# Output projection of a hybrid attention/SSD layer: four token blocks interleaved over each weight block, two at the start of the second half of the columns

## The chip, the cores and the metric

The kernel runs on one core of a Trainium2 chip. A core has five engines with an instruction stream each: TensorE (PE, with its weight loads PEld), VectorE (DVE), ScalarE (ACT), GpSimd (POOL) and SyncE (SP), whose queue issues the DMA transfers here. Matmuls write their sums into PSUM, which has eight banks of 128 x 512 values of 32 bits; other data lies in SBUF. The metric is the device time of one execution in microseconds, as the median of several runs.

## The reference

One layer over 1024 tokens of width 1024: a combined input projection, differential attention, a Mamba-2 SSD branch, and at the end the two branches are merged by gates and projected back.

```python
merged = jax.nn.sigmoid(g_a) * (y_a @ w_proj_attn) + jax.nn.sigmoid(g_s) * (y_s @ w_proj_ssd)
return x + (merged @ w_out).astype(x.dtype)
```

All of it is float32. The change concerns only the last product, `merged @ w_out`, of 1024 x 1024 by 1024 x 1024, and the addition of x.

## The kernel before, in words

A float32 operand is split into a high and a low part of a faster format (F32R): ScalarE writes the high part, VectorE or GpSimd subtracts it for the low part (`act` at L224, `tt` at L232). A product is then three matmuls, high x high, high x low, low x high (`steps3`), all recorded by `mm` at L198.

The program records its instructions through a planner (`Plan`): tasks are Python generators that run in an order set by modelled costs and due times, and each engine executes what was recorded for it in that order. Waits between engines are semaphores set by the framework from the real uses of the buffers. The planner decides the order, the chip decides the times.

The stages before the projection are the three products that give `merged` (`products`, tiles pX, pY, pZ, with the gates gl and the partial results ac). `merged` stands transposed, in blocks of 128 channels by 512 tokens: `mgs[kb, half]`, kb from 0 to 7, each with high and low part. They lie in whatever buffers were free, so in the rows they are called mg, hH or hL; for a part of them an `acc_d` block is read back and split in place.

The projection is `final`. Its loop is over two halves n of the 512 output columns; in each, over eight token blocks t of 128; in each, over the eight weight blocks kb of 128 rows by 512 columns. One weight block is one tile `w` with a high and a low part; w136 to w143 are those of the first half, w144 to w151 those of the second. There are nine buffers for them and four for the raw weights as loaded (`raw`). A token block sums 8 x 3 = 24 matmuls in one PSUM bank (`po` + n + t + part), and `out_evac` then has VectorE multiply by 0.5 and add the block of x (`xr`, L240), which is stored from there (`out`). The last block of all is done in two parts of 256 columns. The weight buffers of a half come free (`w_done`) while its last token block, t = 7, passes. `XAHEAD` = 3 blocks of x are loaded ahead. PSUM banks are handed out from one ring of eight (`trs`).

Of the kernel before, what the change touches and what calls it, by code (L numbers as in the profile page):

```python
# [15 lines left out]
P = 128  # L16
S = 1024
D = 1024
KB = D // P
NT = S // P  # L20
# [15 lines left out]
ZF, ZH = {5: 2, 9: 3}, {}  # L36
WPOOL = 3
XAHEAD = 3
HOP = 0.12
INF = float("inf")  # L40

# [36 lines left out]
class Plan:  # L78
# [8 lines left out]
    def op(self, eng, cost, after, shared=False):  # L87
# [3 lines left out]
        if shared:  # L91
            self.e["L"] = s + cost
        return s + cost + HOP

# [44 lines left out]
def tile_hybrid_layer(ctx: ExitStack, tc: tile.TileContext, x, norm_w, w_in, q_norm_w, k_norm_w,  # L139
# [26 lines left out]
    pl = Plan()  # L166
    bigs, mids, sms = Slots(NBIG), Slots(NMID), Slots(NSM)
    trs, qlos = Slots(8), Slots(2)
# [8 lines left out]
    def midt(shape=(P, 512), dt=F32, name="m"):  # L177
        return mid.tile(list(shape), dt, tag="b2", name=name)
# [7 lines left out]
    def trt(name):  # L186
        return ps_tr.tile([P, 512], F32, tag="tr", name=name)

    mmt = trt
# [7 lines left out]
    def mm(o, lhsT, rhs, start, stop, after=0.0, **kw):  # L197
        nc.tensor.matmul(o, lhsT=lhsT, rhs=rhs, start=start, stop=stop, **kw)  # L198
        n, m = rhs.free_size(), lhsT.free_size()
        if rhs.dtype == F32:  # L200
            c = max(4 * n / 2400, 0.215)
        else:
            c = max(n / 2400 + lag[0], 0.057 if m <= 64 else 0.107)
        pl.t = max(pl.t, after) + c
# [5 lines left out]
    def pe_done():  # L210
        return pl.t + 0.2
# [11 lines left out]
    def act(o, i, f, after, **kw):  # L223
        nc.scalar.activation(o, i, f, **kw)  # L224
        if f in (AF.Silu, AF.Exp) and f != table[0]:
            table[0] = f
            pl.op("A", 1.3, after)
        c = 0.83e-3 * i.free_size() + (0.052 if in_ps(i) else 0.093) + 0.093 * (("accum_out" in kw) + any(not isinstance(kw.get(i, 0.0), float) for i in ("scale", "bias")))
        return pl.op("A", c, after)

    def tt(o, a, b, op, after, eng="V"):
        (nc.vector if eng == "V" else nc.gpsimd).tensor_tensor(out=o, in0=a, in1=b, op=op)  # L232
        n = o.free_size()
        if eng == "G":
            return pl.op("G", 0.095 + (1.85e-3 if op == ALU.mult else 2.3e-3) * n, after, True)
        sb = not in_ps(a, b)
        return pl.op("V", 0.07 + 0.07 * sb + 1.042e-3 * n, after, sb)

    def stt(o, a, s, b, op0, op1, after):
        nc.vector.scalar_tensor_tensor(out=o, in0=a, scalar=s, in1=b, op0=op0, op1=op1)  # L240
        sb = not in_ps(a, b)
        return pl.op("V", 0.07 + 0.07 * sb + 1.042e-3 * o.free_size() + (0.0 if isinstance(s, float) else 0.06), after, sb)
# [9 lines left out]
    def load(o, i, after=0.0):  # L252
        nc.sync.dma_start(out=o, in_=i)  # L253
        q = pl.op("Q", 0.48, max(after, pl.t))
        n = o.free_size() * 512 / 360e3 if o.space != bass.MemoryType.DRAM else i.free_size() * 512 / 360e3
        return pl.op("D", n, q + 0.6) + lag[1]
# [218 lines left out]
    def w_next(n):  # L475
        i = used[0]
        used[0] += n
        return list(range(i, i + n))

    def w_need(i):  # L480
        while i not in w_at:
            yield pl.t + 0.1
        while w_at[i] > pl.t:
            yield w_at[i]

    def w_done(i):
        ws.give(w_slot[i], pl.t + 0.1)
        wts.pop(i)

    def wide(i):  # L490
        return wts[i][:, 0].rearrange("p f c -> p (f c)"), wts[i][:, 1].rearrange("p f c -> p (f c)")
# [5 lines left out]
    def steps3(o, a, b, first, last, **kw):  # L497
        mm(o, a[0], b[0], first, False, **kw)
        yield
        mm(o, a[0], b[1], False, False, **kw)  # L500
        yield
        mm(o, a[1], b[0], False, last, **kw)
        yield
# [22 lines left out]
    def form_evac(t):  # L526
# [16 lines left out]
        def split(f, src, at):  # L543
# [4 lines left out]
            for kp in range(2):  # L548
                at = tt(forms_t[f, 1, kp][0][:, :, cs], src[:, 2 * kp:2 * kp + 2], forms_t[f, 0, kp][0][:, :, cs],
                        ALU.subtract, at - HOP if kp else at)  # L550
            forms_at[f] = at
# [20 lines left out]
    def prep_h(t):  # L572
# [24 lines left out]
        for i in range(2):  # L597
            hs = slice(i * 512, i * 512 + 512)
            at = stt(xt[:, hs], xt[:, hs], rs, nwb[i], ALU.mult, ALU.mult, at - HOP if i else at)
            nt.append(at)  # L600
# [10 lines left out]
    def h_evac(t, half, pt, kt, at):  # L611
# [5 lines left out]
        if t >= 4:  # L617
            km = yield from pl.get(mids)
            b = midt([P, 4, P], name=f"b{half + 1}2{t}")
            t1 = act(b, src, AF.Copy, at - HOP)  # L620
            sums12[t, half] = (b, km, t1)
# [86 lines left out]
    def qk_stack(h, half, qk):  # L708
# [10 lines left out]
        for isk in range(2):  # L719
# [17 lines left out]
            for m, (own, other) in enumerate(((lo, hi), (hi, lo))):  # L737
                if isk:
                    t1 = tt(kk[m][other, cs], pt[own], kk[m][own, cs], ALU.subtract, t1 - HOP)
                else:  # L740
                    t1 = stt(ql[own, m], pt[own], wqk_c[own], qh[own, m], ALU.mult, ALU.subtract, t1 - HOP)
            done.append(t1)
# [651 lines left out]
    forms, mgs = {}, {}  # L1394
# [233 lines left out]
    def final():  # L1628
        outs = [(n, t) for n in range(2) for t in range(NT)]
        for i in range(XAHEAD):  # L1630
            pl.spawn(load_xr(*outs[i]))
        for n in range(2):
            ids = w_next(KB)
            for t in range(NT):
                if n * NT + t + XAHEAD < len(outs):
                    pl.spawn(load_xr(*outs[n * NT + t + XAHEAD]))
                tsl = slice(t % 4 * P, (t % 4 + 1) * P)
                parts = 2 if (n, t) == (1, NT - 1) else 1
                for i in range(parts):
                    wsl = slice(i * 512 // parts, (i + 1) * 512 // parts)  # L1640
                    k = yield from pl.get(trs, first=True)
                    pm = mmt(f"po{n}{t}{i}")
                    for kb in range(KB):
                        yield from w_need(ids[kb])
                        while (kb, t // 4) not in mgs:
                            yield pl.t + 0.1
                        mg, at = mgs[kb, t // 4]
                        if at > pl.t:
                            yield at
                        wh, wl = wide(ids[kb])  # L1650
                        yield from steps3(pm[:, wsl], (mg[:, 0, tsl], mg[:, 1, tsl]), (wh[:, wsl], wl[:, wsl]),
                                          kb == 0, kb == KB - 1)
                        if t == NT - 1 and i == parts - 1:
                            w_done(ids[kb])
                    pl.spawn(out_evac(pm, k, xrs[n, t], slice(t * P, (t + 1) * P), n * 512, wsl, i == parts - 1), pe_done())

    xrs = {}

    def load_xr(n, t):
        xrs[n, t] = cell = []  # L1660
        km = yield from pl.get(mids)
        xt = midt(name=f"xr{n}{t}")
        cell += [xt, km, load(xt, xv[t * P:(t + 1) * P, n * 512:n * 512 + 512])]

    def out_evac(pm, k, cell, rows, c0, wsl, last):
        at = pe_done()
        while len(cell) < 3:
            yield pl.t + 0.1
        xt, km, tx = cell
        at = max(at, tx)  # L1670
        yield at
        at = stt(xt[:, wsl], pm[:, wsl], 0.5, xt[:, wsl], ALU.mult, ALU.add, at)
        trs.give(k, at)
        yield at
        at = load(ov[rows, c0 + wsl.start:c0 + wsl.stop], xt[:, wsl], at)
        if last:
            mids.give(km, at)
# [7 lines left out]
    def bulk():  # L1685
        pl.spawn(ssd_all())
        pl.spawn(prepare())
        step = {"z": ssd_proj_z, "h": att_proj}
        for kind, i in ORDER1:
            if kind in "cg":  # L1690
                yield from front_pair(kind, i, (kind, i) == FPAIRS[-1])
            elif kind in step:
                yield from step[kind](i)
            else:
                yield from dt_proj() if kind == "dt" else att_setup()
        pl.spawn(fill())
        yield from gates()
        lag[:] = [0.0135, 2.5]
        for c in range(3):
            yield from products(c)  # L1700
        yield from final()
# [58 lines left out]
```

## Time and profile before

| | us |
|---|---|
| median of 3 runs (1653.99 to 1654.98) | 1654.75 |
| the profiled execution, its own time | 1649.99 |
| its span, from the first to the last instruction | 1648.3 |
| TensorE busy in that span | 1598.3 |
| mean granted clock of TensorE, as a share of full | 0.992 |

The profile is of one further execution; its span is 1.69 us shorter than its own time, and its time is 4.76 us below the median of the runs. Matmuls are pipelined: a row's duration is longer than the distance to the next one's start, so the pace is read from starts. TensorE's granted clock has two levels, 1.2 and 2.4 GHz; 1.00 in a row of the windows is the upper one, 0.50 the lower.

### The profile page before, as it was taken

Reading aid. Unit: us, or ns where it says so; the run is one execution under the profiler, and the core shown is the slowest. Engines: PE = TensorE matmul, PEld = TensorE weight load, DVE = VectorE, ACT = ScalarE, POOL = GpSimd, SP = SyncE. Lnnn points to the kernel's source line nnn. Section 1 sums busy time; section 2 is a strip of 40 time slices with the busy share of each in tenths; the row PEclk is TensorE's granted clock in tenths of the full one; section 3 lists DMA queues with packets and bytes.
Section 4 is the critical chain, followed back from the end, with each engine's and each line's share of the span. In section 5 each row is a group of like instructions: output and inputs, shape, how many; then the busy total and the mean of one; then the engine's idle time right before and its main releaser. Section 6 shows DMA issues by size and latency. Waiting matters only on the chain. (4 is left out here: it accounts for less than half of the span.)

```text
span 1648.3 us, 24347 instructions
## 1 busy us (share of the span) xinstructions
PE 1598.3 (97%) x8010; PEld 1332.0 (81%) x8010; DVE 1082.8 (66%) x2011; ACT 911.5 (55%) x2215; POOL 701.8 (43%) x847
## 2 busy tenths in 40 slices
PE   7999999999999999999999999999999999989899
PEld 5788888888788888887878888888787887777687
DVE  7836568447782676876777877776656657796821
ACT  7534457455663557786666877676665625252410
POOL 4315455235541545456475555464665233313100
PEclk9999999999999999999999999999999999999999
DMA  6213343524452361426253514242425649596832
GB/s 207 91 57 107 108 150 107 168 87 118 132 187 82 107 203 56 129 70 180 83 192 122 152 50 133 71 156 88 145 86 190 225 132 373 184 332 205 273 128 71
DMA packets 223804, 236.47 MB, mean 143 GB/s; under 512 B 15285, under 2 KB 155326, under 8 KB 223678
## 3 DMA queue, kind: packets, MB, share of 16 engines
q1 hardware_dynamic: 223678, 234.93, 44.8%
q8 instruction: 63, 1.03, 0.3%
q14 instruction: 63, 0.52, 0.1%
HBM read 164.48 MB, written 70.39 MB: 142 GB/s over the span
## 5 line engine op out<-in xcount | busy, mean ns | idle before, releaser
L198 PE MATMUL pma<-w,hH 128*128 128x512 f32 x1024 | 346.1, 406 | 5.6 <-POOL w L232 5.4
L232 POOL TENSOR_TENSOR rawf<-rawf,rawf 128x512 f32<-128x512 f32 x90 | 121.4, 1349 | 257.6 <-DVE wp L232 110.3
L198 PEld LDWEIGHTS pma<-w,hH 128*128 128x128 f32 x1024 | 189.2, 190 | 40.4 <-POOL w L232 6.6
L198 PE MATMUL pma<-w,hL 128*128 128x512 f32 x512 | 207.5, 405 | 0.0
L224 ACT ACTIVATE wp<-rawf 128x512 fp32r<-128x512 f32 x180 | 109.4, 625 | 103.3 <-POOL rawf L232 70.3
L198 PE MATMUL pmz<-w,hH 128*128 128x512 f32 x512 | 164.3, 398 | 0.7 <-ACT hH L224 0.6
L232 DVE TENSOR_TENSOR wp<-rawf,wp 128x512 fp32r<-128x512 f32 x144 | 110.5, 787 | 55.9 <-ACT wp L224 55.7
L224 ACT ACTIVATE w<-raw 128x512 fp32r<-128x512 f32 (+1 forms) x122 | 74.8, 626 | 80.1 <-PE po L198 35.9
L224 ACT ACTIVATE p<-p,nm 128x256 f32<-128x256 f32 (+7 forms) x128 | 98.6, 773 | 32.5 <-DVE nm L771 31.7
L198 PEld LDWEIGHTS pmz<-w,hH 128*128 128x128 f32 x512 | 96.5, 190 | 20.7 <-ACT hH L224 1.0
L198 PEld LDWEIGHTS pma<-w,hL 128*128 128x128 f32 x512 | 97.3, 190 | 16.3 <-issue 0.2
L198 PE MATMUL fYc<-ft,wp 128*128 128x512 f32 x432 | 106.5, 392 | 0.7 <-DVE fu L232 0.7
L232 POOL TENSOR_TENSOR w<-raw,w 128x512 fp32r<-128x512 f32 (+1 forms) x38 | 51.5, 1355 | 124.7 <-ACT w L224 124.6
L198 PE MATMUL pmz<-w,hL 128*128 128x512 f32 x256 | 101.3, 396 | 0.0
L198 PEld LDWEIGHTS fYc<-ft,wp 128*128 128x128 f32 x432 | 81.1, 189 | 18.0 <-DVE fu L232 1.1
L232 POOL TENSOR_TENSOR s<-rawf,rawf 128x512 f32<-128x512 f32 x30 | 40.5, 1351 | 118.8 <-DMA rawf<-in_w_proj_ssd_dram 56.1
L232 DVE TENSOR_TENSOR w<-raw,w 128x512 fp32r<-128x512 f32 (+1 forms) x84 | 67.1, 810 | 23.0 <-ACT w L224 22.6
L224 ACT ACTIVATE ab<-ab,nac 128x128 f32<-128x128 f32 x256 | 78.4, 393 | 1.7 <-POOL ab L1174 1.5
L198 PEld LDWEIGHTS av<-v,at 128*128 128x128 f32 x576 | 72.8, 191 | 6.5 <-ACT at L224 2.6
L264 POOL TENSOR_TENSOR rs<-rs,mhalf 128x4 f32<-128x4 f32 (+1 forms) x71 | 75.3, 1061 | 5.9
L771 DVE CUSTOM_DVE_ANT_0 p<-sc,maskb 128x512 f32<-128x512 f32 (+3 forms) x128 | 72.1, 585 | 8.4 <-issue 4.0
L198 PE MATMUL av<-v,at 128*128 128x128 f32 x576 | 75.1, 275 | 1.5 <-ACT at L224 1.5
(301 smaller groups left out, 4074.7 us busy)
## 6 DMA issues: line engine op xcount, KB each, us to landing
raw<-in_w_in_dram SPq DMA_DIRECT2D x104, 256.0 KB, 3.5
rawf<-in_w_in_dram SPq DMA_DIRECT2D x72, 256.0 KB, 3.9
ab<-act_d SPq DMA_DIRECT2D x32, 512.0 KB, 4.7
cv_d<-cv SPq DMA_DIRECT2D x48, 256.0 KB, 2.2
t_d<-ts SPq DMA_DIRECT2D x24, 512.0 KB, 3.2
z_d<-zs SPq DMA_DIRECT2D x32, 256.0 KB, 2.0
xr<-cv_d SPq DMA_DIRECT2D x32, 256.0 KB, 3.1
zc<-z_d SPq DMA_DIRECT2D x32, 256.0 KB, 3.1
```

The costliest lines, as they stand in the source:

```text
L198: nc.tensor.matmul(o, lhsT=lhsT, rhs=rhs, start=start, stop=stop, **kw)
L224: nc.scalar.activation(o, i, f, **kw)
L232: (nc.vector if eng == "V" else nc.gpsimd).tensor_tensor(out=o, in0=a, in1=b, op=op)
L264: nc.gpsimd.tensor_tensor(out=dst, in0=dst, in1=mhalf[:, 0:cols], op=ALU.pow)
L771: nc.vector.tensor_tensor_reduce(out=p[:, j:e], in0=sc[i][:, 0:e - j], in1=maskb[:, S - n + j:S - n + e], scale=-1.0, scalar=nms[i - 1] if ...
```

## The change

In each half of the columns the token blocks are now taken in groups (`FINAL_T`): in the first half blocks 0 to 3 as one group and then 4 to 7 singly, in the second half blocks 0 and 1 as one group and then 2 to 7 singly. In a group each block has a PSUM bank of its own, and the loop over weight blocks is outside that over the group's token blocks: a weight block is used by all of them before the next is needed. The blocks of x for a whole group are asked for at the group's start. Each block is evicted after its own last matmul. The number of matmuls, loads, splits and stores stays the same.

```diff
+FINAL_T = (((0, 1, 2, 3), (4,), (5,), (6,), (7,)), ((0, 1), (2,), (3,), (4,), (5,), (6,), (7,)))
...
-            for t in range(NT):
-                if n * NT + t + XAHEAD < len(outs):
-                    pl.spawn(load_xr(*outs[n * NT + t + XAHEAD]))
-                tsl = slice(t % 4 * P, (t % 4 + 1) * P)
-                parts = 2 if (n, t) == (1, NT - 1) else 1
+            for ts in FINAL_T[n]:
+                for t in ts:
+                    if n * NT + t + XAHEAD < len(outs):
+                        pl.spawn(load_xr(*outs[n * NT + t + XAHEAD]))
+                parts = 2 if (n, ts[-1]) == (1, NT - 1) else 1
                 for i in range(parts):
                     wsl = slice(i * 512 // parts, (i + 1) * 512 // parts)
-                    k = yield from pl.get(trs, first=True)
-                    pm = mmt(f"po{n}{t}{i}")
+                    pms = []
+                    for t in ts:
+                        k = yield from pl.get(trs, first=True)
+                        pms.append((trt(f"po{n}{t}{i}"), k))
                     for kb in range(KB):
                         yield from w_need(ids[kb])
...
+                        for t, (pm, k) in zip(ts, pms):
...
+                            yield from steps3(pm[:, wsl], (mg[:, 0, tsl], mg[:, 1, tsl]), (wh[:, wsl], wl[:, wsl]),
+                                              kb == 0, kb == KB - 1)
+                            if kb == KB - 1:
+                                pl.spawn(out_evac(pm, k, xrs[n, t], slice(t * P, (t + 1) * P), n * 512, wsl, i == parts - 1),
+                                         pe_done())
+                        if ts[-1] == NT - 1 and i == parts - 1:
                             w_done(ids[kb])
-                    pl.spawn(out_evac(pm, k, xrs[n, t], slice(t * P, (t + 1) * P), n * 512, wsl, i == parts - 1), pe_done())
```

TensorE, at the start of the projection, before: one bank (po000, token block 0) takes all eight weight blocks in turn, then the next bank begins.

```order
L198 MATMUL po000_16120<-w136_16040,hH_111 128x512 x3
L198 MATMUL po000_16120<-w137_16051,hL_112 128x512 x3
L198 MATMUL po000_16120<-w138_16067,hH_111 128x512 x3
L198 MATMUL po000_16120<-w139_16079,hL_112 128x512 x3
L198 MATMUL po000_16120<-w140_16156,hH_111 128x512 x3
L198 MATMUL po000_16120<-w141_16159,hL_112 128x512 x3
L198 MATMUL po000_16120<-w142_16162,mg60_16056 128x512 x3
L198 MATMUL po000_16120<-w143_16165,hL_112 128x512 x3
L198 MATMUL po010_16190<-w136_16040,hH_111 128x512 x3
```

The same place of the change: a weight block goes through four banks, po000 to po030, before the next one.

```order
L199 MATMUL po000_16120<-w136_16040,hH_111 128x512 x3
L199 MATMUL po010_16121<-w136_16040,hH_111 128x512 x3
L199 MATMUL po020_16122<-w136_16040,hH_111 128x512 x3
L199 MATMUL po030_16123<-w136_16040,hH_111 128x512 x3
L199 MATMUL po000_16120<-w137_16051,hL_112 128x512 x3
L199 MATMUL po010_16121<-w137_16051,hL_112 128x512 x3
L199 MATMUL po020_16122<-w137_16051,hL_112 128x512 x3
L199 MATMUL po030_16123<-w137_16051,hL_112 128x512 x3
L199 MATMUL po000_16120<-w138_16067,hH_111 128x512 x3
```

So the first use of w140 moves from the 13th matmul of the stage to the 49th, and that of w143 from the 22nd to the 85th.

SP's queue behind the loads of w140 to w143's raw weights, before (raw144 to raw147 are the first four weight blocks of the second half, xr the blocks of x, out_0_dram the stores):

```order
L253 DMA raw143_16102<-in_w_out_dram 128x512
L253 DMA xr00_16123<-in_x_dram 128x512
L253 DMA xr01_16125<-in_x_dram 128x512
L253 DMA xr02_16127<-in_x_dram 128x512
L253 DMA xr03_16129<-in_x_dram 128x512
L253 DMA raw144_16170<-in_w_out_dram 128x512
L253 DMA raw145_16175<-in_w_out_dram 128x512
L253 DMA raw146_16180<-in_w_out_dram 128x512
L253 DMA raw147_16185<-in_w_out_dram 128x512
L253 DMA xr04_16192<-in_x_dram 128x512
L253 DMA out_0_dram<-xr00_16123 128x512
```

The same place of the change:

```order
L254 DMA xr03_16132<-in_x_dram 128x512
L254 DMA xr04_16134<-in_x_dram 128x512
L254 DMA xr05_16136<-in_x_dram 128x512
L254 DMA xr06_16138<-in_x_dram 128x512
L254 DMA raw144_16210<-in_w_out_dram 128x512
L254 DMA raw145_16218<-in_w_out_dram 128x512
L254 DMA raw146_16223<-in_w_out_dram 128x512
L254 DMA raw147_16228<-in_w_out_dram 128x512
L254 DMA raw148_16252<-in_w_out_dram 128x512
L254 DMA out_0_dram<-xr00_16126 128x512
L254 DMA out_0_dram<-xr01_16128 128x512
```

Three loads of x stand ahead of raw144 that stood behind raw147 before. On TensorE everything ahead of the projection stands as it stood; on ScalarE, VectorE and GpSimd the whole order is the same (each weight split, merged split and eviction at its old place).

## Rows read from the trace of the kernel before

**Rows 1.** The page: the span, and TensorE's busy time, share and instructions.

```profile
span 1648.3 us, 24347 instructions
PE 1598.3 (97%) x8010; PEld 1332.0 (81%) x8010; DVE 1082.8 (66%) x2011; ACT 911.5 (55%) x2215; POOL 701.8 (43%) x847
```

**Rows 2.** TensorE's waits from 1405 us on: releaser, total, times, longest.

```profile
PE po L198 <- DVE w L232: 3.1, 1, 3.1
PE po L198 <- ACT w L224: 2.4, 1, 2.4
```

**Rows 3.** The chain that ended last, its end: start, us, what.

```profile
1557.55 0.61 DVE w L232
...
1558.20 86.61 PE po L198 x395
...
1644.84 0.42 DVE xr L240
```

**Rows 4.** Timeline of TensorE in the projection: start, us, operation, count, idle before.

```profile
1549.31 0.84 PE L198 MATMUL po<-w,hH 128*128 128x512 f32 x3
...
1554.56 0.50 PE L198 MATMUL po<-w,hH 128*128 128x512 f32 x1 [2.36 <-ACT w L224]
1558.20 1.22 PE L198 MATMUL po<-w,hH 128*128 128x512 f32 x2 [3.14 <-DVE w L232]
1559.22 1.48 PE L198 MATMUL po<-w,hL 128*128 128x512 f32 x3
1560.50 1.48 PE L198 MATMUL po<-w,mg 128*128 128x512 f32 x3
...
1562.69 0.85 PE L198 MATMUL po<-w,hH 128*128 128x512 f32 x3
...
1595.34 4.24 PE L198 MATMUL po<-w,mg 128*128 128x512 f32 x18
...
1606.24 0.84 PE L198 MATMUL po<-w,hH 128*128 128x512 f32 x3
```

**Rows 5.** Windows: busy time and count of each engine, TensorE's clock, DMA share, GB/s.

```profile
1050.43:1052.51 2.08, 2.08 (x10) 1.69 (x9) 1.64 (x6) 1.47 (x4) 0.73 (x2) 1.00 0.04 8
...
1549.30:1552.10 2.80, 2.80 (x13) 2.06 (x11) 2.77 (x6) 2.80 (x6) 0.00 (x0) 1.00 1.00 326
1559.22:1560.50 1.28, 1.28 (x4) 0.99 (x3) 0.73 (x2) 0.63 (x1) 0.08 (x1) 0.50 0.61 198
1562.70:1600.80 38.10, 38.10 (x170) 31.56 (x169) 7.43 (x10) 2.53 (x4) 1.30 (x1) 1.00 0.40 129
```

**Rows 6.** Timelines of ScalarE, VectorE and GpSimd: the splits of the weights.

```profile
1553.88 2.64 ACT L224 ACTIVATE w<-raw 128x512 fp32r<-128x512 f32 x4
1559.71 0.63 ACT L224 ACTIVATE w<-raw 128x512 fp32r<-128x512 f32 x1 [2.10 <-DMA raw<-in_w_out_dram]
...
1557.46 1.89 DVE L232 TENSOR_TENSOR w<-raw,w 128x512 fp32r<-128x512 f32 x3
1559.27 0.68 DVE L232 TENSOR_TENSOR hH<-gl,hH 128x512 fp32r<-128x512 f32 x1
...
1555.23 1.51 POOL L232 TENSOR_TENSOR w<-raw,w 128x512 fp32r<-128x512 f32 x1 [10.03 <-ACT w L224]
```

**Rows 7.** Timeline of SP's queue: start, us of issuing, transfer, count.

```profile
1548.68 2.31 SPq L253 DMA_DIRECT2D raw<-in_w_out_dram  x4
1551.22 2.32 SPq L253 DMA_DIRECT2D xr<-in_x_dram  x4
```

**Rows 8.** Timeline of TensorE in the attention stage: from one sc to another, to pO, pS and pma.

```profile
1050.43 0.39 PE L198 MATMUL sc<-kk,qlo 128*128 128x512 f32 x1
...
1051.13 0.39 PE L198 MATMUL pO<-sh,ch 128*128 128x512 f32 x1
...
1051.82 0.39 PE L198 MATMUL pS<-xh,bT 128*128 128x512 f32 x1
...
1052.51 0.39 PE L198 MATMUL pma<-w,hH 128*128 128x512 f32 x1
```

More of the change, by code (lines that the diff above doesn't have):

```diff
@@ L1639, in final @@
                 for i in range(parts):
                     wsl = slice(i * 512 // parts, (i + 1) * 512 // parts)
-                    k = yield from pl.get(trs, first=True)
-                    pm = mmt(f"po{n}{t}{i}")
+                    pms = []
+                    for t in ts:
+                        k = yield from pl.get(trs, first=True)
+                        pms.append((trt(f"po{n}{t}{i}"), k))
                     for kb in range(KB):
                         yield from w_need(ids[kb])
[L1645 to L1649, printed above, removed]
-                        wh, wl = wide(ids[kb])
-                        yield from steps3(pm[:, wsl], (mg[:, 0, tsl], mg[:, 1, tsl]), (wh[:, wsl], wl[:, wsl]),
-                                          kb == 0, kb == KB - 1)
-                        if t == NT - 1 and i == parts - 1:
+                        wh, wl = wide(ids[kb])
+                        for t, (pm, k) in zip(ts, pms):
+                            while (kb, t // 4) not in mgs:
+                                yield pl.t + 0.1
+                            mg, at = mgs[kb, t // 4]
+                            if at > pl.t:
+                                yield at
+                            tsl = slice(t % 4 * P, (t % 4 + 1) * P)
+                            yield from steps3(pm[:, wsl], (mg[:, 0, tsl], mg[:, 1, tsl]), (wh[:, wsl], wl[:, wsl]),
[4 more added lines that the diff above has]
+                        if ts[-1] == NT - 1 and i == parts - 1:
```

## Prediction

> **What bounds the kernel now.** I read the page first. TensorE is busy 97% of a span of 1648.3 us [rows 1], so the time is that of TensorE's stream plus the places where it stands still. The chain of waits, followed back from the end, shows which place counts for this change: from 1558.20 us to the end it is nothing but the output projection's matmuls, 86.61 us of them, with one eviction of 0.42 us behind, and what released the chain's first matmul is a VectorE split of a weight block that ran until 1558.16 [rows 3]. The waits of TensorE in the last part of the program name the same spot: 3.1 us for VectorE and 2.4 us for ScalarE, once each, both on the projection's weights [rows 2]. So a microsecond won at the start of this stage is a microsecond won at the end.
>
> The timeline of TensorE gives the size. A token block is 24 matmuls (8 weight blocks, 3 each). Blocks 1 to 6 of the first half take (1595.34 - 1562.69) / 6 = 5.44 us each, 0.227 us a matmul. Block 0 begins at 1549.31 and block 1 at 1562.69: 13.38 us. The reader is to see in [rows 4] where it goes: one matmul of the fifth weight block only at 1554.56 (the engine sat 2.36 us), the next two at 1558.20 (3.14 us), and from there three matmuls in 1.28 us (1559.22 to 1560.50), 0.427 each. The windows say why those are slow: the granted clock is 1.00 before the gap, 0.50 in that stretch, which is 1.2 GHz in place of 2.4, and 1.00 again from 1562.70 [rows 5]. Block 0 thus costs 13.38 - 5.44 = **7.94 us** too much: 5.50 of idle time, and 2.4 for the matmuls at or near the lower clock.
>
> Why it waits: the fifth to eighth weight blocks (w140 to w143) are ready late. ScalarE converts the four from 1553.88 on, VectorE makes the low parts of three of them in 1557.46 to 1559.35, GpSimd one in 1555.23 to 1556.74 [rows 6]. Both engines are busy with splits of the merged activations before, in an order that the change leaves alone.
>
> **The change part by part.** *The first half's first four blocks go together.* Each weight block now feeds 12 matmuls, 12 x 0.227 = 2.72 us, before the next is needed. The four blocks that are ready at the start (before, they run without a gap from 1549.31) cover 48 matmuls, 10.88 us. So w140's high part is wanted at 1549.31 + 10.88 = 1560.19, its low part one matmul later at 1560.42, and w141 to w143 at 1562.9, 1565.6 and 1568.4. In the trace TensorE took up w140's low part at 1558.20, w141's was made at 1556.74, and the other two by 1559.35 [rows 4, 6]. Every one is early, the tightest by 1560.42 - 1558.20 = **2.2 us**. No gap, so nothing before which the clock could fall: the whole 7.94 us goes. What is late next? Block 4 needs the second token half's last activation, split by VectorE in 1559.27 to 1559.95 [rows 6]; it is wanted after 96 matmuls, at 1571.07 plus six weight blocks. Nothing there.
>
> *Four PSUM banks in turn.* The output bank now changes every 3 matmuls and a bank is resumed with an open sum: 32 runs of three in the first group against 4 runs of 24, and 16 against 2 in the second half's pair, 42 more changes. No stage before does just this. Below: block 0's neighbours change bank at 5.44 us a block with no excess, so 0. Above: in the attention stage nine matmuls of 512 columns go through four changes of bank (from one score tile sc to another, to pO, to pS, to pma), the last of them back into the open sum of a projection, from 1050.43 to 1052.51, 2.08 us [rows 8], against 9 x 0.227 = 2.04; that is 0.01 us a change, 0.4 for 42. It could not give time back, since the matmuls are the same. I take 0.1, nearer to the block boundaries, which are of this very stage.
>
> The page TensorE: Matmul & The Clock Gate of the Trainium skill, section "A second HAM failure mode: psum-queue depth-cycling", speaks against this edit: it tells of a kernel that cycled through PSUM banks and whose TensorE paused so often between groups that its clock fell again and again. By the row above the 42 changes cost at most 0.4 us; by that rule the two grouped stretches would run at the lower level, which is the third rival below. The granted clock of the nearest row, 1.00 over those nine matmuls, does not agree with it.
>
> *Eviction.* The four results of the group now come 0.68 us apart, not 5.44 apart; VectorE has nothing else to do then, and TensorE goes on into a fifth bank. 0. The first half's last block, which releases the weights, and the last block of all, in two parts, stand as before, so the tail is the same.
>
> *Queues.* On SP's queue the loads of three more residual blocks (xr04 to xr06) now go ahead of the four weight blocks of the second half (w144 to w147), and block 0's store behind a fifth. They go out behind xr03. Before, w140 to w143's loads were issued in 1548.68 to 1550.99 and xr00 to xr03's in 1551.22 to 1553.54 [rows 7], so the three cannot hold up w140, which ScalarE was reading at 1553.88. Three loads at 2.32 / 4 = 0.58 us of issue are 1.7 us of queue for what follows. Of that, w144 comes first; before, ScalarE converted it at 1559.71 [rows 6], and it is wanted when the second half begins, now 1600.78 - 7.94 = 1592.8. Cover 30 us. 0.
>
> *The pair at the second half.* Block 0 of that half runs from 1595.34 + 5.44 = 1600.78 to 1606.24 [rows 4], 5.46 us: there is 0.02 us to win, and the pair halves the pace at which its weights are wanted. 0.
>
> Sum against the profiled execution: 1649.99 - 7.94 + 0.1 = 1642.15 us. The median of the runs, 1654.75, is 4.76 longer than that execution; the same difference on it gives 1654.75 - 7.84 = **1646.9 us**, 0.47% less. A change of 0.2%, 3.3 us, is about what can be told from none.
>
> **The rivals.** *The weights are later, and the gap moves.* If w140 is ready x later in the timed runs than here, the old order loses x more and the new one only x - 2.2: a gain of up to 7.84 + 2.2 = 10.1, 1644.6 us. If everything is earlier, the gain shrinks: with the idle time gone up but no fall of the clock it is 5.5, 1649.3; 5.5 us earlier, nothing. For it: the timed runs are longer somewhere. Against: VectorE's and ScalarE's work ahead of w140 is a fixed list. Gains between 3.3 and 5.5 (1649.3 to 1651.4): chance 0.04; the rest lies in the forecast's range.
>
> *The gain is given back (no change).* It would need something tied to a clock of its own behind block 0 that holds the end where it is. Everything of the second half hangs on TensorE itself (weight slots come free at block 7), or has 30 us of cover, so I find no such thing; that the profiled wait is absent in timed runs is the other way to it. About 1654; chance 0.06.
>
> *The bank changes cost the clock (slower).* If the grouped stretches, 96 + 48 = 144 matmuls, ran at the lower level, 0.427 in place of 0.227 each, they would cost 28.8 us, for a gain of 7.9: 1654.75 + 20.9 = 1675.6. It decides for slower from (7.94 + 3.3) / 144 = 0.078 us of excess a matmul. Against it stands the row of four changes in nine matmuls at 0.231 [rows 8] at a clock of 1.00 [rows 5]. Chance 0.04.
>
> **How the numbers follow.** The forecast has 0.86: 1646.9. Its range runs from a gain of 10.1 less the runs' spread of 1 us, 1643.6, to 1650.5, which takes in the 0.4 for the banks and a good part of the case without a fall of the clock; the rest of the cases is less than 2 in 10. Faster by over 0.2%: 0.86 + 0.04 = 0.90; within: 0.06; slower: 0.04.
>
> **What would show it.** In the new profile: TensorE's matmuls without a gap from the projection's first one on; each run of 12 on one weight block 2.72 us; the clock at 1.00 throughout the stage; block 4's first matmul 21.8 us after the stage's first, at about 1571.1; the second half at about 1592.8, and the end of the span near 1640.4. No row of TensorE waiting for w. The prediction is wrong if a gap appears before w140 or later, if runs of three at a bank change take more than 0.68 us, if the clock falls in a grouped stretch, or if something else takes the end.

## The result and the profile after

The change takes 1644.66 us (median of 9 runs, 1640.33 to 1646.06) against 1654.75 before (9 runs, 1647.51 to 1659.12): a ratio of 0.9936, 95% interval 0.9918 to 0.9953, or 7.8 to 13.6 us less. The forecast was 1646.9 with a range from 1643.6 to 1650.5, and a gain of 7.84.

The page of the profiled execution begins like this:

```profile
span 1644.3 us, 24350 instructions
PE 1598.4 (97%) x8010; PEld 1333.0 (81%) x8010; DVE 1082.8 (66%) x2011; ACT 912.4 (55%) x2215; POOL 702.4 (43%) x847
```

TensorE is busy for the same 1598 us as in [rows 1], and the span is just 4.0 us shorter than before. The reason is seen in the timeline of TensorE in the projection (start, us, operation, count):

```profile
1553.70 2.88 PE L199 MATMUL po<-w,hH 128*128 128x512 f32 x12
1556.42 2.88 PE L199 MATMUL po<-w,hL 128*128 128x512 f32 x12
...
1564.58 2.88 PE L199 MATMUL po<-w,hH 128*128 128x512 f32 x12
...
1572.74 2.88 PE L199 MATMUL po<-w,hL 128*128 128x512 f32 x12
1575.46 4.24 PE L199 MATMUL po<-w,mg 128*128 128x512 f32 x18
...
1608.10 0.84 PE L199 MATMUL po<-w,hH 128*128 128x512 f32 x3
```

The stage begins at 1553.70, in this execution 4.39 us later than in [rows 4], although every engine's order ahead of it is the same. So the two spans can't be compared, but the stages can. I measure a stage from the first projection matmul to the start of the last eviction: before 1549.31 to 1644.84, 95.53 us; now 1553.70 to 1641.25, 87.55 us. The last rows of the chain of waits give that end:

```profile
1553.86 87.36 PE po L199 x408
...
1641.25 0.42 DVE xr L241
```

TensorE's busy time is the same only as a sum of two differences. Up to the stage it was 1508.34 us before and is 1510.85 now, as the windows show (the first is of before, the second of the change; PE's busy time is the second figure). In the stage it was 89.98 and is 87.51, so not only idle time went but slow matmuls too.

```profile
0.00:1549.31 1549.31, 1508.34 (x7602) 1257.51 (x7603) 1056.48 (x1972) 899.65 (x2196) 696.40 (x843) 0.99 0.46 145
0.00:1553.70 1553.70, 1510.85 (x7602) 1259.70 (x7603) 1054.91 (x1972) 901.71 (x2197) 696.46 (x843) 0.99 0.45 145
```

Each weight block now takes 2.72 us (1553.70 to 1556.42), block 4 follows 21.76 us after the first matmul, and no matmul of the projection has an idle time before it. The windows of the first group, of the pair and of the rest show the clock (length, busy time and count of PE, PEld, DVE, ACT, POOL, then TensorE's clock, DMA share, GB/s):

```profile
1553.70:1575.46 21.76, 21.76 (x97) 18.02 (x96) 14.57 (x21) 6.26 (x12) 3.33 (x2) 1.00 0.59 211
1597.20:1608.10 10.90, 10.90 (x49) 9.01 (x48) 2.54 (x4) 1.90 (x3) 1.29 (x1) 1.00 0.36 120
1608.10:1641.20 33.10, 33.10 (x169) 28.23 (x167) 4.78 (x8) 0.00 (x0) 0.00 (x0) 1.00 0.22 76
```

It stays at 1.00; the stretch of 0.50 in [rows 5] has no counterpart. What remained to be explained is the difference between 8.0 us (the stages of the two profiles) and 10.1 (the medians), and which part of the change does what.

### The profile page after: what moved, and what is told of

Same layout as the page of the kernel before. It is cut to its first block, busy times and chain, and to the rows that moved or that the text cites. A ratio compares the mean times of both kernels' runs of the same rounds, so it can differ in the third digit from the quotient of the medians.

```text
span 1644.3 us, 24350 instructions
## 1 busy us (share of the span) xinstructions
PE 1598.4 (97%) x8010; PEld 1333.0 (81%) x8010; DVE 1082.8 (66%) x2011; ACT 912.4 (55%) x2215; POOL 702.4 (43%) x847
```

## The experiments

All but the two further profiles of before, which are one execution each, were timed in turns with the kernel before on the same chip. "Stage" is measured as above.

| kernel | stage, us | idle in it, us | ratio to before | 95% interval |
|---|---|---|---|---|
| before, first profile | 95.53 | 5.50 | | |
| before, second and third profile | 96.64, 96.57 | 6.54 each | | |
| pair only | 96.35 | 6.56 | 0.9996 | 0.9985 to 1.0007 |
| fill | 94.98 | 1.43 | 0.9989 | 0.9975 to 1.0004 |
| first two | 93.55 | 4.12 | 0.9975 | 0.9962 to 0.9988 |
| weights first | 89.80 | 1.68 | 0.9948 | 0.9930 to 0.9966 |
| first three | 89.30 | 1.44 | 0.9952 | 0.9934 to 0.9969 |
| four only | 87.55 | 0 | 0.9935 | 0.9919 to 0.9950 |
| the change | 87.55 | 0 | 0.9936 | 0.9918 to 0.9953 |
| more banks | 87.55 | 0 | 0.9946 | 0.9928 to 0.9964 |
| both cures | 87.55 | 0 | 0.9947 | 0.9928 to 0.9965 |

**How much cover: two and three token blocks**

```diff
-FINAL_T = (((0, 1, 2, 3), (4,), (5,), (6,), (7,)), ((0, 1), (2,), (3,), (4,), (5,), (6,), (7,)))
+FINAL_T = (((0, 1), (2,), (3,), (4,), (5,), (6,), (7,)), ((0,), (1,), (2,), (3,), (4,), (5,), (6,), (7,)))
```

> Only the first two token blocks of the first half go side by side, all others singly. Our theory (the gain is the cover that the group gives to the late weight blocks): w140's low part is wanted 5.67 us after the stage's first matmul and is ready 8.9 to 9.9 us after it, so TensorE still stands 3.2 to 4.2 us, once. From the first projection matmul to the last eviction: 95.5 before, 87.6 with no gap, here 90.8 to 92.0 if the clock holds and up to 2.4 more if it falls; 3.5 to 4.7 or about 2 us faster than before. Rival (what counts is the number of banks or the second half's pair): no difference to before for the pair, or the whole 8 us from two banks.

For the next one the first group is (0, 1, 2), with the second half singly too.

> The first three token blocks of the first half go side by side, all others singly. Our theory: w140's low part is wanted 8.39 us after the stage's first matmul and ready after 8.9 to 9.9: a stand of 0.5 to 1.5 us, too short for the clock to fall. Stage 88.1 to 89.1 us, 6.4 to 7.4 us faster than before, a microsecond short of the change. Rival (four banks needed, or the second half's pair carries part of the gain): clearly less.

TensorE's timeline with two blocks, and then with three (start, us, operation, count, idle before):

```profile
1548.37 1.52 PE L199 MATMUL po<-w,hH 128*128 128x512 f32 x6
...
1553.81 0.39 PE L199 MATMUL po<-w,hH 128*128 128x512 f32 x1
1558.32 1.50 PE L199 MATMUL po<-w,hH 128*128 128x512 f32 x5 [4.12 <-DVE w L233]
1559.61 2.76 PE L199 MATMUL po<-w,hL 128*128 128x512 f32 x6
```

```profile
1551.62 2.20 PE L199 MATMUL po<-w,hH 128*128 128x512 f32 x9
...
1559.78 0.39 PE L199 MATMUL po<-w,hH 128*128 128x512 f32 x1
1561.60 2.12 PE L199 MATMUL po<-w,hH 128*128 128x512 f32 x8 [1.44 <-DVE w L233]
1563.56 2.21 PE L199 MATMUL po<-w,hL 128*128 128x512 f32 x9
```

In both, TensorE takes w140's high part at once and stands at its low part: 4.12 us with two blocks, 1.44 with three. Every block added to the group wins the 2.72 us of four weight blocks' matmuls, and the low part is taken up 9.95 and 9.98 us after the stage's first matmul. Behind the stand of 4.12 us there are six matmuls that take 2.56 us (1559.61 to the next row's 1562.17), 0.427 each; behind that of 1.44 us nine take 2.05, 0.228 each. The windows of these two stretches, with two blocks and then with three, give the granted clock, 0.50 and 1.00:

```profile
1559.61:1562.17 2.56, 2.56 (x7) 1.98 (x6) 1.54 (x1) 0.00 (x0) 0.99 (x1) 0.50 0.36 124
1563.56:1565.61 2.05, 2.05 (x10) 1.69 (x9) 0.90 (x1) 0.00 (x0) 0.35 (x1) 1.00 0.63 209
```

So in these two executions the longer stand cost the clock and the shorter didn't. The stage with three blocks, 89.30 us, is 0.2 above the forecast, the one with two inside it. With four blocks the low part is wanted at 11.11 us, 1.2 after it is ready.

**Which half: the pair alone, the four alone**

> Only the second half's pair of token blocks; the first half as before. Our theory: 0.02 us to win, nothing to be measured against before (ratio 1.000 within 0.2%), and the first token block has its gap of about 5.5 to 6.6 us again. Rival (the pair carries the 2 us by which the timed gain exceeds the 7.94 of the profile): 2 us faster, 0.12%.

> Only the first half's group of four; the second half as before. Our theory: the change's whole gain, 8 to 10 us against before (ratio 0.994 to 0.995), stage 87.5 us without a gap. Rival (the pair carries 2 us of it): 2 us slower than the change.

The pair alone is worth nothing that can be measured (0.9996), and the four alone everything (0.9935, stage 87.55). The gain isn't spread over the two edits.

**The kernel before, profiled again**

> The kernel before, profiled once more. In its first profile w140's low part was taken up 8.9 us after the stage's first matmul; in the change and in all four experiments so far it was ready only after 9.2 to 10.0. If the first profile was a favourable one, the stage here takes some 1 us longer than its 95.5 us, and the timed gain of the change (10.1) and of the others (each 1.5 to 2 us above what their stage shows) is explained by that. If it is 95.5 again, the rest of those gains lies outside the stage or in the spread of the runs.

> The same once more, to see how far the stage of the kernel before varies from execution to execution: 96 to 98 us if the first profile was a favourable one, 95.5 if it was typical.

The first of these expectations is not exact: of the four experiments that it counts, weights first (below) took w140's low part up only 3.9 us after the start, the other three 9.95 to 9.98 after; and the medians of the four exceed what their stages show by 1.4 to 2.4 us. TensorE's timeline of the second profile of before:

```profile
1548.33 0.84 PE L198 MATMUL po<-w,hH 128*128 128x512 f32 x3
...
1552.21 0.49 PE L198 MATMUL po<-w,hH 128*128 128x512 f32 x1 [1.00 <-ACT w L224]
1558.24 1.22 PE L198 MATMUL po<-w,hH 128*128 128x512 f32 x2 [5.54 <-DVE w L232]
...
1562.84 0.86 PE L198 MATMUL po<-w,hH 128*128 128x512 f32 x3
```

Block 0 takes 14.51 us here and 14.42 in the third profile, not the 13.38 of [rows 4]: w140's low part is taken up 9.9 us after the start, not 8.9. The waits of 1.00 and 5.54 us also say more clearly than those of the first profile (2.36 and 3.14) which engine is late: ScalarE's high part is there soon, VectorE's low part isn't. Between the two waits VectorE is without a pause, busy 6.00 us of 6.03, as the window shows:

```profile
1552.21:1558.24 6.03, 0.49 (x1) 0.18 (x1) 6.00 (x9) 2.72 (x5) 1.76 (x1) 0.79 0.51 183
```

So the stage before takes 96.6 us in two of three profiles, and the change wins 9.05 us of that. In the first profile VectorE happened to be 1.1 us faster; why is told at the end.

**The clock alone: the gap filled with matmuls**

```diff
+                        if (n, t, kb) == (0, 0, 4):
+                            spare_bank = trt("pfill")
+                            mg, wh = mgs[0, 0][0], wide(ids[0])[0]
+                            for j in range(NFILL):
+                                nc.tensor.matmul(spare_bank, lhsT=mg[:, 0, tsl], rhs=wh, start=j == 0, stop=j == NFILL - 1)
```

> The order of before, with 24 additional matmuls into a bank that nobody reads, recorded between the fourth and fifth weight block of the first token block; the output does not change. They fill 5.44 us of the gap, so TensorE waits for w140 as long as before but is busy while it waits. If the clock is 2.4 of the 7.94 us, as we worked out, the stage takes 95.5 - 2.4 = 93.1 us and the run is 2.4 us faster than before, with a granted clock of 1.00 behind the gap. Rival (waiting alone makes the loss, the slow matmuls come from something else, such as the weights' arrival): no gain.

TensorE's timeline (L1649 is the added loop):

```profile
1549.40 0.84 PE L199 MATMUL po<-w,hH 128*128 128x512 f32 x3
...
1552.12 5.60 PE L1649 MATMUL pfill<-w,hH 128*128 128x512 f32 x24
1557.56 0.39 PE L199 MATMUL po<-w,hH 128*128 128x512 f32 x1
1559.38 0.73 PE L199 MATMUL po<-w,hH 128*128 128x512 f32 x2 [1.43 <-DVE w L233]
1559.95 0.85 PE L199 MATMUL po<-w,hL 128*128 128x512 f32 x3
```

The window from the end of the wait to the start of token block 1:

```profile
1559.38:1562.26 2.88, 2.88 (x12) 2.09 (x12) 2.85 (x3) 0.00 (x0) 1.68 (x1) 1.00 0.40 100
```

w140 comes as late as ever (9.98 us after the start), but behind it three matmuls take 0.69 us where they took 1.28, at a granted clock of 1.00. The stage is 1.6 us shorter than the 96.6 of before, not 2.4. Part of the 2.4 was never the clock's: read from starts, the eleven matmuls behind the wait took 4.60 us in the second profile of before (1558.24 to 1562.84), against 11 x 0.227 = 2.49, so 2.1 too much. In the fill they take 2.88. The 0.4 by which that still exceeds 2.49 lies in part in a wait that shows up once the matmuls are fast: the three for the last weight block have 0.94 us to the next row in place of 0.68. The timed ratio, 0.9989 (0.9975 to 1.0004), can't tell 1.6 from 2.4 or from nothing; the trace alone carries this.

**The weights earlier, the order of TensorE as before**

```diff
     def fill_mg():
+        goal = used[0] + KB
         for h in range(2):
             for ob in range(6):
+                while h and made[0] < goal:
+                    yield pl.t + 0.2
```

> The order of before on TensorE; the read-back of the second token half's merged blocks (six of eight, wanted only by the fifth token block) waits until the planner has split the eight weight blocks of the first half. That takes six splits each on ScalarE and VectorE from in front of w140 to w143. Our theory (w140 to w143 are late because those splits stand ahead of them): they are ready some 4 us earlier on VectorE (six splits of 0.6) and earlier still on ScalarE; most of the gap of 5.5 us goes, at least 3.6 us, and the clock holds; 5 to 8 us faster than before. Rival (the weights are late because their loads are): no more than 1 us.

TensorE's timeline:

```profile
1551.09 0.84 PE L198 MATMUL po<-w,hH 128*128 128x512 f32 x3
...
1555.00 0.73 PE L198 MATMUL po<-w,hH 128*128 128x512 f32 x2 [0.80 <-DVE w L232]
...
1557.53 0.73 PE L198 MATMUL po<-w,mg 128*128 128x512 f32 x2 [0.88 <-DVE w L232]
```

w140's low part is taken up 3.9 us after the start, 6 us earlier than in the later profiles of before, where some 4 were expected; two short waits remain, of 1.68 us together, and the stage is 6.8 us shorter than 96.6. So lateness of the weights is the cause, and it can be met from either side. The edit moves the loads of w140 to w143 ahead too, so by itself it doesn't tell splits from loads; that the loads were there in time is shown by the second profile of before, where ScalarE had converted all four by 1553.71 while VectorE's first low part began at 1557.51:

```profile
1551.54 2.17 ACT L224 ACTIVATE w<-raw 128x512 fp32r<-128x512 f32 x4
```

```profile
1557.51 2.97 DVE L232 TENSOR_TENSOR w<-raw,w 128x512 fp32r<-128x512 f32 x3
```

**The banks, and both cures together**

More banks has `FINAL_T = (((0, 1, 2, 3), (4, 5, 6), (7,)), ((0, 1, 2, 3), (4, 5, 6), (7,)))`.

> Groups of four (blocks 0 to 3) and three (blocks 4 to 6) in both halves, the last block singly: 56 changes of bank more than in the change, all where no wait is. Our theory (a change of bank costs 0, at most 0.01 us): stage 87.6 us as in the change, at most 88.1, granted clock 1.00, ratio to before as that of the change, 0.993 to 0.995. Rival (cycling through banks makes TensorE pause and its clock fall): the 336 matmuls in groups at up to 0.427 us in place of 0.227, a stage of up to 155 us, slower than before.

> The change, and in addition the read-back of the second token half's merged blocks held back until the eight weight blocks of the first half are split. Our theory: TensorE already runs the stage without a gap, so earlier weights only add cover (w140 some 4 us earlier than in the change): stage 87.6 us, ratio as that of the change. Rival (in some executions the change still waits for w140, since the cover is 1.2 us in our last profiles and not 2.2): a smaller spread and up to 1 us faster than the change.

With 56 more changes of bank the stage is 87.55 us, to a hundredth that of the change. Two rows of TensorE's timeline in the second half's group of four, and a window that spans the second half:

```profile
1599.40 2.88 PE L199 MATMUL po<-w,hL 128*128 128x512 f32 x12
1602.12 2.88 PE L199 MATMUL po<-w,hH 128*128 128x512 f32 x12
```

```profile
1592.00:1640.00 48.00, 48.00 (x234) 40.65 (x233) 10.01 (x15) 4.43 (x7) 2.59 (x2) 1.00 0.34 110
```

With runs of three matmuls of 512 columns, a change of bank costs nothing that the trace shows, and the clock stays at 1.00. Both cures together give 87.55 us too: TensorE has no gap left for the second one to close. The ratios of the three versions lie within each other's intervals, so neither of the two can be told from the change.

## Why the prediction was right

**The place and the size.** The loss was block 0's, as [rows 4] put it, and it went whole: the stage without a gap is 87.55 us in four different kernels. The term of 7.94 us was worked out from an execution in which it was small, and so came out 1.1 us short. Two more profiles give 14.51 - 5.44 = 9.07 and 14.42 - 5.44 = 8.98 us. 9.05 us on 1654.75 is a ratio of 0.9945, inside the measured interval; the 10.1 of the medians differs from it by no more than the runs' spread allows. This was the first half of the first rival (weights later in other executions than in the profile), which the range had taken in. What the prediction held against it, that VectorE's and ScalarE's work ahead of w140 is a fixed list, is true of the list and not of its duration: the same VectorE work took 1.1 us longer in the later profiles (see the last section). Its reason for the lateness, both engines busy, holds for VectorE alone: ScalarE had the four weights converted 3.8 us before VectorE began on them in the second profile.

**The cover.** The forecast said w140 would be the tightest, early by 2.2 us. It was, by 1.2: in the change's profile VectorE made it, the first of the three below (0.68 us each), in 1562.92 to 1563.60, and it was wanted at 1553.70 + 11.11 = 1564.81.

```profile
1562.92 1.89 DVE L233 TENSOR_TENSOR w<-raw,w 128x512 fp32r<-128x512 f32 x3
```

The experiment with three blocks confirms it from the other side: 1.2 less 2.72 is a stand of 1.5, and 1.44 was measured.

**The two parts of the loss.** 5.50 us of idle time and 2.4 of slow matmuls; in the later profiles 6.54 and 2.4 to 2.5. That the second part follows from the first is shown by the trace of the fill: with TensorE busy in the wait, the clock didn't fall. The second part was over-sized. The prediction took the idle time from row ends and gave the rest to the clock; from starts, the eleven matmuls of [rows 4] from 1558.20 to 1562.69 are 2.0 us too slow, and the stand is 5.9. The fill brought back 1.6.

**The banks.** I allowed 0.1, with 0.4 as the upper bound from the attention stage [rows 8]. It is 0.00, the lower bound. The third rival is out: 0.227 us a matmul and a clock of 1.00 with a change every three matmuls. What the Trainium skill tells of a kernel that cycles through PSUM banks (TensorE: Matmul & The Clock Gate, "A second HAM failure mode: psum-queue depth-cycling"), pauses between the groups of matmuls and a clock that falls again and again, does not occur in this trace. No run here shows what made the other kernel pause.

**Queues, evictions, the second half.** Costed at nothing, and nothing is what they show: no wait of TensorE in the stage, and a ratio of 0.9996 for the pair alone.

**What was off.** The absolute times: block 4 was foretold for 1571.1 and the end of the span for 1640.4; they came at 1575.46 and 1644.3, because the stage itself began 4.39 us later (what follows the last eviction was 0.4 us shorter). The distances inside the stage were right to 0.1 us. In twelve profiled executions that share TensorE's order up to the stage, it began between 1548.33 and 1554.63, so the span of one profile against that of another is no measure for a change of this size. The traces show what most of this scatter goes with: the time for which TensorE's granted clock stood at 0.50 ahead of the stage. With 20.5 us of it the stage began at 1548.3 to 1549.3 (three executions, the first profile of before among them), with 23.9 at 1550.4 to 1551.6 (five), with 27.3 at 1553.2 to 1554.6 (three, the change's among them). The fill, with 13.7 and 1549.4, doesn't fit. Why that time differs between executions stays open.

## What to carry to other kernels

Where an operand arrives in pieces at a stage's start, let each piece do all the work that it can before the next is needed; the number of results kept open decides how much lateness it hides, here 2.72 us for each more bank. Compare the lateness with the cover in several profiles, not one: here they were 8.9 and 9.9 us against 11.1, and one bank less would have left a gap. And time a stage from its own first instruction, not from the start of the span.

## What the runs showed of the hardware that was not expected

What made VectorE 1.1 us faster in the first profile of before is seen beside GpSimd's low part of w141. In the second profile GpSimd works on it while VectorE splits four merged blocks, both from SBUF:

```profile
1551.50 3.56 DVE L232 TENSOR_TENSOR mg<-mg 128x512 fp32r<-128x512 f32 x4
```

```profile
1552.75 1.76 POOL L232 TENSOR_TENSOR w<-raw,w 128x512 fp32r<-128x512 f32 x1 [8.57 <-ACT w L224]
```

In the first, ScalarE converted w141 later: just ahead of the weights it waited 0.82 us for a merged block to be read back, as it didn't in the second. GpSimd began at 1555.23 [rows 6], and the same four splits were through before it:

```profile
1552.53 2.49 DVE L232 TENSOR_TENSOR mg<-mg 128x512 fp32r<-128x512 f32 x4
```

3.56 us against 2.49 is 1.1 us, the whole difference. The three weight splits of VectorE show the same again, 2.97 us beside a GpSimd subtraction in the second profile and 1.89 without in [rows 6]. So an operation of GpSimd on SBUF held VectorE back by 1.1 us, and whether it fell on an operation of VectorE that could be held differed from execution to execution. The twelve traces together bear this out. They hold 4932 VectorE subtractions of this shape. The 3363 that began while GpSimd ran nothing took at most 0.70 us each. All 601 that took more than 0.80, up to 1.83, began while an operation of GpSimd ran, and they ended 0.54 to 0.56 us after it did, whenever they had begun. This is read from the overlap in the traces; no run changed GpSimd's share of the splits to show it.
